# A diffusion block on one Trainium2 core: fewer and reordered first loads, the last sum of squares behind a weight split and a dot product, three dot products moved to a later stage, and an exponential table loaded ahead

## The chip, the core and the metric

The kernel runs on one core of a Trainium2 chip. The core has a matrix engine (PE in the profile; its weight loads, which overlap the matmuls, are PEld), VectorE (DVE), ScalarE (ACT), GpSimd (POOL) and SyncE (SP). Transfers between HBM and the core's memory are issued by an engine's queue, here nearly all by SP's, and are carried by 16 DMA engines. Each engine works through its own instructions in order, and waits for others by semaphores.

The metric is the device time of one execution in microseconds (us). Before the change three runs took 1520.72, 1521.96 and 1522.29 us; their median, 1521.96 us, is the time to compare with.

## The reference

One layer of a diffusion backbone: 256 latent tokens `x` and 256 context tokens `ctx`, width 2048, all float32. Cut to what matters here:

```python
mod = silu(c) @ w_mod + b_mod            # 6 x 2048: shifts, scales, gates; the same from c_ctx
h  = rms_norm(x, g_pre) * (1 + sc1) + sh1
hc = rms_norm(ctx, g_pre) * (1 + csc1) + csh1
# one projection w_in gives queries, keys and values of two mixers and two gates
oa = window attention with sinks (8 heads, 2 key heads, rotary)   # keys of h and hc
ob = neighbourhood attention (8 heads, relative bias)             # keys of h and hc
y  = (sigmoid(ga) * (oa @ w_br_a) + sigmoid(gb) * (ob @ w_br_b)) @ w_o
x  = x + gt1 * rms_norm(y, g_post)
x  = x + gt2 * rms_norm(conv_ffn(modulated rms_norm(x)), g_ffn_post)
```

The context enters only as keys and values. Every row of `w_mod` (2048 by 12288) is used once, against one or two vectors, so that part of the work is loading.

## The kernel before, in words

**Precision.** A float32 operand is split into two parts, a high one (`hi`, a rounded copy that ACT writes) and a low one (`lo = src - hi`, by DVE). A product is then three matmuls: high by high, low by high, high by low. `split` (L123) writes both parts; `halves` (L134) does it for a weight block of 128 by 2048 in two pieces, and leaves its last ACT and DVE instruction in `last`. So each weight block costs ACT and DVE two instructions each before PE can use it.

**Weights** arrive as raw blocks of 1024 KB or less in a ring of four buffers (`raw_block`, L113, tag `raw`). `load_to` issues the loads in the order in which the blocks are used, `block` (L162) splits one block ahead and loads two or three ahead. A buffer is free again when the block's low part has been made. The split parts have a ring of two (tags `wh`, `wl`), so the split of a block waits until PE has finished the block two before it.

**Dot products.** The parts of `w_mod` that aren't matmuls are multiply-and-sum instructions of DVE over 128 by 2048 elements: `dot` (L385) for the first shift columns, `beside` (L581) for the biases that the shifts give to the keys, and `mods` (L194), which takes one row block of `w_mod` (`wm_b`, 1024 KB through the same four raw buffers), and loads the next one ahead. 48 of these `mods` have to be done before the normalisation behind the attention, and 16 in the up projection.

**Stages.** The order of the work is that of the program text, planned by the language's scheduler with its own estimates, except where `manual_schedule` keeps the written order (PE up to L547, SP up to L439) and where `issue_after` puts an instruction behind another one on the same engine.

1. *Start.* SP issues, in order, `ccol` (16 KB, L101), the first scale block `wm_sc[0]` in four pieces (L278), the columns `cols` (80 KB, L291), the first input tile `xn` (256 KB), the first key weights `wk[0]` in three pieces (L293), `wm_sc[1]`, `wk[1]`, `xn[1]`. PE multiplies the identity with itself (`keep_busy`, L232) until `narrow` (L303) turns the scale block into 128 scale values, `evacuated` copies them (ACT), two small matmuls turn them into columns, and `scale_of` (L321) makes the column `Gc` (DVE) and the scaled input `hx`, `hc` in two parts (ACT, DVE).
2. *First keys,* the loop over k at L415: for each of 16 slices of the width, 36 matmuls add to six key heads (`keys`, L399). Inside, every second slice, the next two scale blocks are turned into scales and inputs, and `squares` (L341) adds the squares of two slices to `ssq` (one ACT instruction, two DVE additions). At k = 11 it is called for slices 12 and 13 and, in the same place, for 14 and 15 (L469), and behind them ACT loads the table for the square root (L471). At k = 12 the weights of slice 13 are split (`unit`, L364) and the first `dot` is placed. At k = 13 one matmul sums `ssq` over the partitions (L474), and `rstd_of` makes the inverse root.
3. *Second keys* (L493): four more key heads, and the shift columns.
4. *Values* (L602): three column groups in ten weight blocks numbered `nb`; beside them DVE does the key biases and then `mods`, 29 steps in all: 3 or 4 for a block, 1 for the last (L609).
5. *Queries and attention* (L669 to L767): per head a query block (`fill`), the scores, softmax with Exp on ACT, transposes and the product with the values. Before the loop two heads' queries are made (L747 to L753).
6. *Gates and branches* (L785): for each j of 16 output strips two gate blocks and one branch block, with `mods` one per gate, and one more beside the branch block at j of 4, 8, 11 and 13 (L799).
7. Output projection, first norm, up projection with convolution and gate, down projection, second norm.

Of the kernel before, what the change touches and what calls it, by code (L numbers as in the profile page):

```python
# [15 lines left out]
P = 128  # L16
# [42 lines left out]
def layer_kernel(ctx, tc, xc, xt, ccol, crow, wm_sc, wm_sd, wm_sh, wm_b, cols, wk, wkt, ws, rope, mask_a, bias_b, out):  # L59
# [41 lines left out]
    sync.dma_start(out=c2, in_=ccol)  # L101
# [138 lines left out]
    with ExitStack() as mx:  # L240
# [3 lines left out]
        with ExitStack() as at:  # L244
# [31 lines left out]
            def load_sc(k):  # L276
                if k < KT:
                    rsc[k] = raw_block(wm_sc[k], parts=1 if k else 4)  # L278
# [10 lines left out]
            load_sc(0)  # L289

            sync.dma_start(out=col[:, :C_CW], in_=cols[:, :C_CW])  # L291
            load_xn(0, 1)
            raws[0] = raw_block(*srcs[0], parts=3)  # L293
            load_sc(1)
            load_to(1)
            load_xn(1, 1)
# [17 lines left out]
            def evacuated(k, n, pm):  # L314
                ev = up.tile([P, 2 * P], F32, tag="half", bufs=2, name=f"ev{k}")
                e_ = nc.scalar.activation(ev[:, : n * P], pm[:, : n * P], AF.Copy)
                if k < 5:
                    queue[k] = (e_.ins, e_.ins)
                return ev

            def scale_of(k, n, ev):  # L321
# [11 lines left out]
                for t in range(k, k + n):  # L333
                    for v in range(2):
                        h_, x_, g_ = hh[v][:, t], xn[:, t, v * S : v * S + S], Gc[:, t, v : v + 1]
                        a_ = nc.scalar.activation(h_[:, 0], x_, AF.Copy, scale=g_)
# [4 lines left out]
            def squares(k, after):  # L341

                sq = sp.tile([P, 2, T2], F32, tag="sq", bufs=2, name=f"sq{k}")
                with tc.issue_after(after):
                    nc.scalar.activation(sq[:], xn[:, k : k + 2], AF.Square)
                if k:
                    nc.vector.tensor_tensor(out=sq[:, 0], in0=sq[:, 0], in1=sq[:, 1], op=ALU.add)
# [15 lines left out]

            def unit(u):  # L364
# [7 lines left out]
                for q in range(0, n, step):  # L372
                    split(h[:, q : q + step], h[:, n + q : n + q + step], raw[:, o + q : o + q + step], queue.get((u, q), queue.get(u)))
# [11 lines left out]
            def dot(after=None):  # L385
                t, v = divmod(ndot[0], 2)
                ndot[0] += 1
                with ExitStack() as es:
                    if after:
                        es.enter_context(tc.issue_after(after))  # L390
                    nc.vector.scalar_tensor_tensor(
                        out=rsd[t][:] if v else junk, in0=rsd[t][:], scalar=1.0, in1=shrow[v], op0=ALU.mult, op1=ALU.mult,
                        accum_out=sh0[:, t, v : v + 1])
                if v:
                    nc.vector.tensor_scalar(
                        out=shc[:, :, t], in0=sh0[:, t], scalar1=col[:, C_BMOD + t : C_BMOD + t + 1], scalar2=None, op0=ALU.add)
                    load_sd(t + 1)

# [12 lines left out]
            scale_of(0, 1, ev)  # L411
# [3 lines left out]
            for k in range(KT):  # L415
# [26 lines left out]
                if k in (12, 14):  # L442
                    dot(after)
                for i in range(NK1):
# [15 lines left out]
                    if n and i == first + 1:  # L460
# [7 lines left out]
                        if k == 11:  # L468
                            after = squares(14, done[0])  # L469
                            with tc.issue_after(done[0]):  # L470
                                warm_table(AF.Sqrt, "k", eps[:, 0:1])  # L471
# [131 lines left out]
            for c, (n0, nw, per) in enumerate(((0, 512, 4), (512, 512, 4), (1024, 256, 8))):  # L603
                pv = [acc(f"pv{c}_{i}") for i in range(4)]
                for g in range(KT // per):
                    wh, wl = block(2)
                    for kk in range(per):

                        if nb and kk < (1 if nb == 9 else 3 if nb % 2 else 4):  # L609
# [142 lines left out]
            fill(0)  # L752
            fill(1)  # L753
# [31 lines left out]
        for j in range(KT):  # L785
# [13 lines left out]
            mods(1 if j in (4, 8, 11, 13) else 0, crb[:])  # L799
# [376 lines left out]
```

## Time and profile before

| what | us |
|---|---|
| median of three runs | 1521.96 |
| the profiled execution | 1524.59 |
| its span (first to last instruction) | 1522.8 |
| PE busy | 1506.0 |
| PE's weight loads busy | 1318.1 |
| DVE busy | 1130.9 |
| ACT busy | 784.4 |

The profile is of one execution, taken by the hardware profiler. Times in it count from the start of the span. A timeline row gives the start, the duration, the engine, the line of the kernel and, in brackets, how long the engine stood idle before and what it waited for; rows of a queue carry a q behind the engine's name. A chain row gives start, duration and the work that the end of the run goes back to. A row of the waits gives the sum, the number and the longest of one kind of wait. A row of stretches gives the bounds, the length, the busy time of each engine with its number of instructions, the granted PE clock (1.00 is full speed), the share of the 16 DMA engines' time in use, and GB/s.

### The profile page before, as it was taken

The numbers are of one execution on the slowest core, as the hardware profiler recorded it, in microseconds if no ns is written. First come the engines' busy times: TensorE is split into PE (matmuls) and PEld (weight loads), VectorE is DVE, ScalarE is ACT, GpSimd is POOL, SyncE is SP. The second block draws the span as 40 slices with busy tenths as digits, with TensorE's granted clock in tenths as the row PEclk, the third lists the DMA queues.
The fourth block names the chain that finished last, engine by engine and source line by source line (L and its number), as shares of the span: only waits on it lengthen the run. The fifth ranks groups of instructions, "written<-read, shape, count | busy, mean of one in ns | idle before, by whom it ended". The sixth has DMA issues, their size and how long they took to land.

```text
span 1522.8 us, 22640 instructions
## 1 busy us (share of the span) xinstructions
PE 1506.0 (99%) x9044; PEld 1318.1 (87%) x9044; DVE 1130.9 (74%) x1673; ACT 784.4 (52%) x1280; POOL 1.6 (0%) x10
## 2 busy tenths in 40 slices
PE   8999999999999999999999999999999999999998
PEld 7988889899988888888888888888888888888886
DVE  3487797888888989887778887888888776444444
ACT  4342542676774445454476555555555555344342
POOL 0000000000000000000000000000000000000000
PEclk9999999999999999999999999999999999999999
DMA  9978778733358888888955666666666556655552
GB/s 350 389 271 328 291 283 326 265 112 130 136 204 322 329 325 337 332 327 317 380 218 195 248 233 237 248 231 221 243 246 235 208 194 234 235 194 193 193 194 83
DMA packets 59833, 382.19 MB, mean 251 GB/s; under 512 B 6608, under 2 KB 7376, under 8 KB 17488
## 3 DMA queue, kind: packets, MB, share of 16 engines
q1 hardware_dynamic: 59152, 379.70, 67.5%
q8 instruction: 71, 1.16, 0.3%
q10 hardware_dynamic: 576, 1.05, 0.2%
q14 instruction: 34, 0.28, 0.0%
HBM read 376.48 MB, written 4.24 MB: 250 GB/s over the span
## 4 chain that ended last, share of the span: by engine, by line
PE 94%; DMA 3%; DVE 2%; ACT 1%; issue 1%; SPq 0%; DVEq 0%; ACTq 0%
PE pu L174 21%; PE py_d L827 16%; PE pu L175 11%; PE pk L403 7%; PE pg L174 7%; PE py_o L827 5%; PE pv L616 5%; PE pq L174 4%; PE pb L174 4%; PE pg L175 4%; PE pb L175 2%; PE pq L175 2%; DMA raw<-in_wm_b_dram 2%; PE po L742 2%; PE s L712 1%; PE pm L309 1%
## 5 line engine op out<-in xcount | busy, mean ns | idle before, releaser
L131 DVE TENSOR_TENSOR wl<-raw,wh 128x1024 fp32r<-128x1024 f32 x444 | 529.4, 1221 | 232.6 <-ACT wh L127 232.4
L127 ACT ACTIVATE wh<-raw 128x1024 fp32r<-128x1024 f32 x444 | 453.1, 1054 | 293.1 <-PE py_d L827 129.0
L174 PE MATMUL pu<-h,wh 128*128 128x512 f32 x1408 | 488.5, 390 | 0.0
L175 PE MATMUL pu<-h,wl 128*128 128x256 f32 x1408 | 396.9, 282 | 0.0
L174 PEld LDWEIGHTS pu<-h,wh 128*128 128x128 f32 x1408 | 264.3, 188 | 55.5 <-DVE h L960 0.2
L175 PEld LDWEIGHTS pu<-h,wl 128*128 128x128 f32 x1408 | 266.1, 189 | 0.1
L827 PE MATMUL py_d<-wh,ff 128*128 128x512 f32 x704 | 216.8, 389 | 0.0
L174 PE MATMUL pg<-hx,wh 128*128 128x512 f32 x464 | 161.5, 390 | 0.0
L827 PEld LDWEIGHTS py_d<-wh,ff 128*128 128x128 f32 x704 | 132.1, 188 | 27.4
L204 DVE SCALAR_TENSOR_TENSOR raw<-raw,crb 128x2048 f32<-128x2048 f32 x64 | 146.2, 2285 | 9.3 <-DMA raw<-in_wm_b_dram 8.0
L827 PE MATMUL py_d<-wl,ff 128*128 128x512 f32 x352 | 136.9, 389 | 0.0
L175 PE MATMUL pg<-hx,wl 128*128 128x256 f32 x464 | 130.8, 282 | 0.0
L403 PE MATMUL pk<-hx,ku 128*128 128x256 f32 x480 | 117.8, 287 | 2.3 <-DVE ku L131 1.9
L403 PE MATMUL pk<-hc,ku 128*128 128x256 f32 x480 | 114.8, 281 | 0.0
L179 ACT ACTIVATE half_u<-pu 128x256 f32<-128x256 f32 x88 | 33.6, 384 | 152.7 <-PE pu L175 152.7
L174 PE MATMUL pq<-hx,wh 128*128 128x512 f32 x304 | 108.6, 396 | 0.0
L174 PEld LDWEIGHTS pg<-hx,wh 128*128 128x128 f32 x464 | 87.1, 188 | 18.2
L403 PEld LDWEIGHTS pk<-hx,ku 128*128 128x128 f32 x480 | 90.5, 189 | 7.7 <-issue 4.7
L403 PEld LDWEIGHTS pk<-hc,ku 128*128 128x128 f32 x480 | 90.7, 189 | 1.3 <-DVE hc L337 0.8
L174 PE MATMUL pb<-oab,wh 128*128 128x512 f32 x256 | 89.4, 390 | 0.0
L175 PEld LDWEIGHTS pg<-hx,wl 128*128 128x128 f32 x464 | 87.7, 189 | 0.0
L175 PE MATMUL pq<-hx,wl 128*128 128x256 f32 x304 | 85.7, 282 | 0.8 <-DVE wl L131 0.8
(184 smaller groups left out, 1937.8 us busy)
## 6 DMA issues: line engine op xcount, KB each, us to landing
raw<-in_ws_dram SPq DMA_DIRECT2D x222, 1024.0 KB, 4.9
raw<-in_wm_b_dram SPq DMA_DIRECT2D x64, 1024.0 KB, 5.1
raw<-in_wm_sc_dram SPq DMA_DIRECT2D x15, 1024.0 KB, 7.9
raw<-in_wm_sh_dram SPq DMA_DIRECT2D x16, 768.0 KB, 7.0
raw<-in_wkt_dram SPq DMA_DIRECT2D x10, 1024.0 KB, 5.5
crb<-sild SPq DMA_DIRECT2D x6, 1024.0 KB, 6.7
raw<-in_wk_dram SPq DMA_DIRECT2D x7, 768.0 KB, 8.4
sd<-in_wm_sd_dram SPq DMA_DIRECT2D x4, 1024.0 KB, 9.0
```

Of the source, the lines that this page charges most:

```text
L127: a_ = nc.scalar.activation(hi, src, AF.Copy)
L131: v_ = nc.vector.tensor_tensor(out=lo, in0=src, in1=hi, op=ALU.subtract)
L174: nc.tensor.matmul(pt[:, :], wh[:, w], a, start=first and i == 0, stop=False, skip_group_check=True)
L175: nc.tensor.matmul(pt[:, :S], wl[:, w], a[:, 0], start=False, stop=last and i == n - 1, skip_group_check=True)
L179: a_ = nc.scalar.activation(t[:], pt[:, S:], AF.Copy)
L204: nc.vector.scalar_tensor_tensor(out=r, in0=r, scalar=1.0, in1=row, op0=ALU.mult, op1=ALU.mult, accum_out=modx[:, j : j + 1])
L309: nc.tensor.matmul(pm[32 * j : 32 * j + 32, t * P : t * P + P], cc[:, q, :], rsc[k + t][:, q * P : q * P + P], start=q < 4, stop=q >= KT - ...
L403: nc.tensor.matmul(pk[:, v * S : v * S + S], wt[:, w], hh[v][:, k, a], start=k == 0 and a == 0 and wt is wh and v == 0, stop=k == KT - 1 a ...
L616: nc.tensor.matmul(pv[i][:, :nw], src[:, k, a, t0 : t0 + P], wt[:, w], start=k == 0 and q == 0, stop=k == KT - 1 and q == 2)
L712: nc.tensor.matmul(s_ps[:], qs[hd][:, a, qt * P : qt * P + P], k_[:], start=q == 0, stop=q == 2)
L742: nc.tensor.matmul(po[:, :S], v_[:, b], pTs[hd][:, b, a], start=b == 0 and q == 0, stop=b == 3 and q == 2)
L827: nc.tensor.matmul(py[t][:], act[:, k, a, t * P : t * P + P], wt[:, w], start=k == 0 and q == 0, stop=k == nk - 1 and q == 2)
```

## The change

- `ccol` is issued by ACT's queue and not by SP's. `wm_sc[0]` comes in two pieces in place of four, `wk[0]` in one in place of three and ahead of `cols` and `xn`; `xn[1]` comes ahead of `wk[1]`.
- In the start, the first `hx` is put behind the first `evacuated` on ACT, and the last third of the first weight split behind the first inputs.
- The squares of slices 14 and 15 move from k = 11 to k = 12, behind the split of the weights of slice 13: ACT's square behind ACT's part of that split, then the square-root table; on DVE the order is split, `dot`, additions. At k = 13 the copy of the last scales (ACT) is put behind the weight split of slice 14.
- In the values, block 8 has two steps beside it in place of four, and block 9 none in place of one: 26 steps, so three `mods` fewer. In the branches, j of 6, 9 and 10 have one `mods` more.
- One ACT instruction with Exp, and so its table load, is put behind the weight split of the second query block, ahead of the attention loop.

```diff
-    sync.dma_start(out=c2, in_=ccol)
+    nc.scalar.dma_start(out=c2, in_=ccol)
...
-                    rsc[k] = raw_block(wm_sc[k], parts=1 if k else 4)
+                    rsc[k] = raw_block(wm_sc[k], parts=1 if k else 2)
...
             load_sc(0)
+            load_to(0)
 
             sync.dma_start(out=col[:, :C_CW], in_=cols[:, :C_CW])
             load_xn(0, 1)
-            raws[0] = raw_block(*srcs[0], parts=3)
             load_sc(1)
+            load_xn(1, 1)
             load_to(1)
-            load_xn(1, 1)
...
             def evacuated(k, n, pm):
                 ev = up.tile([P, 2 * P], F32, tag="half", bufs=2, name=f"ev{k}")
-                e_ = nc.scalar.activation(ev[:, : n * P], pm[:, : n * P], AF.Copy)
+                with ExitStack() as es:
+                    if k == KT - 2:
+                        es.enter_context(tc.issue_after(done_u[k][0]))
+                    e_ = nc.scalar.activation(ev[:, : n * P], pm[:, : n * P], AF.Copy)
...
-                        a_ = nc.scalar.activation(h_[:, 0], x_, AF.Copy, scale=g_)
+                        with ExitStack() as es:
+
+                            if v == k == 0:
+                                es.enter_context(tc.issue_after(queue[0][0]))
+                            a_ = nc.scalar.activation(h_[:, 0], x_, AF.Copy, scale=g_)
...
-            def squares(k, after):
+            sq_ = []
+
+            def squares(k, after, behind=None):
...
-                    nc.scalar.activation(sq[:], xn[:, k : k + 2], AF.Square)
+                    sq_[:] = [nc.scalar.activation(sq[:], xn[:, k : k + 2], AF.Square).ins]
                 if k:
-                    nc.vector.tensor_tensor(out=sq[:, 0], in0=sq[:, 0], in1=sq[:, 1], op=ALU.add)
+                    with ExitStack() as es:
+                        if behind:
+                            es.enter_context(tc.issue_after(behind))
+                        nc.vector.tensor_tensor(out=sq[:, 0], in0=sq[:, 0], in1=sq[:, 1], op=ALU.add)
...
-                    split(h[:, q : q + step], h[:, n + q : n + q + step], raw[:, o + q : o + q + step], queue.get((u, q), queue.get(u)))
+                    done_u[u] = split(
+                        h[:, q : q + step], h[:, n + q : n + q + step], raw[:, o + q : o + q + step], queue.get((u, q), queue.get(u)))
...
-            scale_of(0, 1, ev)
+            done = scale_of(0, 1, ev)
+            queue[0, 4 * P] = done[:2]
...
-                if k in (12, 14):
+                if k == 12:
+
+                    d_ = dot(done_u[k + 1][1])
+                    after = squares(14, done_u[k + 1][0], d_)
+                    with tc.issue_after(sq_[0]):
+                        warm_table(AF.Sqrt, "k", eps[:, 0:1])
+                if k == 14:
                     dot(after)
...
-                        if k == 11:
-                            after = squares(14, done[0])
-                            with tc.issue_after(done[0]):
-                                warm_table(AF.Sqrt, "k", eps[:, 0:1])
...
-                        if nb and kk < (1 if nb == 9 else 3 if nb % 2 else 4):
+                        if nb and kk < (0 if nb == 9 else 2 if nb == 8 else 3 if nb % 2 else 4):
                             beside(1)
...
             fill(0)
+            with tc.issue_after(last[0]):
+                warm_table(AF.Exp, "e", eps[:, 0:1])
             fill(1)
...
-            mods(1 if j in (4, 8, 11, 13) else 0, crb[:])
+            mods(1 if j in (4, 6, 8, 9, 10, 11, 13) else 0, crb[:])
```

(`dot` now also returns its DVE instruction, so that others can be put behind it.)

More of the change, by code (lines that the diff above doesn't have):

```diff
@@ L362, in load_unit @@
                         in_=wk[k : k + 2, :, NK1 * P :].rearrange("k p n -> p k n"))
+            done_u = {}
             def unit(u):
@@ L390, in dot @@
                         es.enter_context(tc.issue_after(after))
-                    nc.vector.scalar_tensor_tensor(
+                    d_ = nc.vector.scalar_tensor_tensor(
                         out=rsd[t][:] if v else junk, in0=rsd[t][:], scalar=1.0, in1=shrow[v], op0=ALU.mult, op1=ALU.mult,
-                        accum_out=sh0[:, t, v : v + 1])
+                        accum_out=sh0[:, t, v : v + 1]).ins
                 if v:
@@ L397, in dot @@
                     load_sd(t + 1)
+                return d_
             def keys(pk, wh, wl, o, k):
```

## The prediction, made before the changed kernel was run

> **What bounds the kernel now.** I read the page first: which engine has no room.
>
> ```profile
> PE 1506.0 (99%) x9044; PEld 1318.1 (87%) x9044; DVE 1130.9 (74%) x1673; ACT 784.4 (52%) x1280; POOL 1.6 (0%) x10
> ...
> L204 DVE SCALAR_TENSOR_TENSOR raw<-raw,crb 128x2048 f32<-128x2048 f32 x64 | 146.2, 2285 | 9.3 <-DMA raw<-in_wm_b_dram 8.0
> ...
> raw<-in_wm_b_dram SPq DMA_DIRECT2D x64, 1024.0 KB, 5.1
> ```
>
> PE is busy in 1506.0 of 1522.8 us, and the change takes no matmul away. So it can win only the 16.8 us in which PE stands still, and what a lowered PE clock costs. The second view is therefore PE's waits:
>
> ```profile
> PE pk L403 <- DVE ku L131: 1.9, 1, 1.9
> PE pm L309 <- DMA raw<-in_wm_sc_dram: 1.6, 2, 0.9
> PE ptx L940 <- DVE yg L930: 1.4, 2, 1.0
> PE s L712 <- ACT q L127: 1.3, 1, 1.3
> PE pq L175 <- DVE wl L131: 0.8, 1, 0.8
> PE pk L403 <- ACT hx L336: 0.4, 1, 0.4
> ```
>
> The diff touches five of these six: the first key weights (0.4), the two scale blocks (1.6), the weights of slice 13 (1.9), the second query block (0.8) and the second query (1.3). The third row, in the norm, stays, as does the end of the run. After each of these waits PE runs without a gap to the next one, so what is won there lasts to the end, unless a new wait takes it back. I go through the places in order of price.
>
> **The wait at slice 13.** The timelines of DVE and of ACT, then the chain of waits around it:
>
> ```profile
> 82.26 0.68 DVE L347 TENSOR_TENSOR sq<-sq 128x512 f32<-128x512 f32 x1
> 82.98 0.69 DVE L348 TENSOR_TENSOR ssq<-ssq,sq 128x512 f32<-128x512 f32 x1
> 83.58 2.29 DVE L391 SCALAR_TENSOR_TENSOR kT<-sd,crb 128x2048 f32<-128x2048 f32 x1
> 85.80 0.95 DVE L131 TENSOR_TENSOR ku<-raw,ku 128x768 fp32r<-128x768 f32 x1
> ```
>
> ```profile
> 79.85 1.99 ACT L345 ACTIVATE sq<-xn 128x1024 f32<-128x1024 f32 x2
> 81.86 1.28 ACT L95 ACT_TABLE_LOAD   x1
> 83.26 0.83 ACT L127 ACTIVATE ku<-raw 128x768 fp32r<-128x768 f32 x1
> ```
>
> ```profile
> 74.02 1.89 PE pm L309 x64
> 75.90 0.90 PE pk L403 x6
> ...
> 86.81 0.50 PE pk L403 x2
> 87.31 2.99 PE pm L309 x64
> 90.30 1.40 PE pk L403 x6
> ...
> 93.54 0.86 PE pss L474 x2
> ```
>
> ```profile
> 84.88:86.81 1.93, 0.00 (x1) 0.01 (x1) 1.87 (x3) 0.00 (x0) 0.00 (x0) 1.00 0.84 265
> ...
> 87.24:91.31 4.07, 4.07 (x70) 3.67 (x70) 0.00 (x0) 0.96 (x2) 0.00 (x0) 0.58 0.87 260
> ```
>
> PE stops at 84.88 for 1.93 us, for the low part of slice 13's weights. ACT makes the high part only at 83.26, behind two squares and the table load; DVE puts the squares' additions and a dot product of 2.29 us ahead of the low part. Right behind the wait the granted clock is 0.58 in a stretch of 4.07 us: 64 matmuls take 2.99 for 1.89, the next six 1.40 for 0.90. That is 1.10 + 0.50 = 1.60 us more (by the clock, 0.42 x 4.07 = 1.71). The place costs 1.93 + 1.6 = about 3.55 us.
>
> With the new order ACT has one square ahead of the split, so the high part starts near 80.9 and ends at 81.7. DVE is then free at 82.26, and the low part is done by 83.2, 1.7 us ahead of PE's need at 84.88. Behind it come the dot product (to 85.5) and the last two additions (82.26 to 83.58 took 1.32, so to 86.8). What waits for that is the matmul over `ssq`: it stands at 93.54, and without stall and slow clock at 93.54 - 3.55 = 90.0. 3.2 us of cover. The table load ends near 84.2 and has nothing of PE behind it, since the weights of slice 14 can't be split before PE leaves slice 12. The last raw and square buffers come free up to 2 us later on SP's queue, but their loads are used only in the next stage. I take the whole 3.55; from below 0, if the wait only moves (first rival); from above 3.7.
>
> The page "TensorE: Matmul & The Clock Gate" of the Trainium skill (Part 1, and its table of goals) puts the fall to half speed behind an idle window of about 3.4 us, and advises against gaps over about 3 us. Here the clock fell behind 1.93 us, so the measurement decides; by the rule as written only 1.93 of the 3.55 would belong to this wait. The page also calls its window free-running, by which the same short wait need not always cost the clock, and the clock can fall without it (a rival below).
>
> **The query stage.** ACT's timeline, and one row of the chain:
>
> ```profile
> 274.76 0.63 ACT L127 ACTIVATE k<-kT 128x512 fp32r<-128x512 f32 x1 [2.81 <-DVE raw L204]
> ...
> 285.47 1.06 ACT L127 ACTIVATE wh<-raw 128x1024 fp32r<-128x1024 f32 x1 [0.57 <-DMA raw<-in_ws_dram]
> ...
> 288.49 1.28 ACT L721 ACT_TABLE_LOAD   x1
> ...
> 291.58 0.40 ACT L127 ACTIVATE q<-rq 128x256 fp32r<-128x256 f32 x1
> ```
>
> ```profile
> 275.60 9.84 DMA raw<-in_ws_dram
> ```
>
> PE's rows give the two waits as 0.8 and 1.3 us. For the first one: ACT stood idle 2.81 us until the ninth `mods` of the values was done, and split the key and the next block only then. With six `mods` in place of nine that wait is gone, and the split comes about 2.8 us earlier, more than 0.8. For the second: `q` is late because the table load of 1.28 stands in ACT's row, and because a weight block landed 9.84 us after its issue, behind `wm_b` blocks. Three blocks fewer are 3 x 1.05 MB, at 410 GB/s (the row for 10 to 27 us below) 7.7 us of loading that no longer stands ahead of it. 1.28 and 0.57 are already more than 1.3; and the 0.8 that PE comes earlier is covered by the 2.81. So up to 2.1 us; I take 2.0, from below 1.3 (the second wait's price alone). The Exp table then loads in a stretch in which PE has a whole query block to work on (as much as a third of the strip of 16.64 us below), and ACT the 2.81 us that it gains; its price is nothing while that holds, at most 1.28.
>
> **The start.** Rows of SP, then PE, then the chain, then stretches:
>
> ```profile
> 1.17 1.84 SPq L120 DMA_DIRECT2D raw<-in_wm_sc_dram  x4
> ```
>
> ```profile
> 7.13 0.43 PE L309 MATMUL pm<-raw,cc 128*32 128x128 f32 x8 [0.70 <-DMA raw<-in_wm_sc_dram]
> ...
> 9.62 0.39 PE L403 MATMUL pk<-hx,ku 128*128 128x256 f32 x1 [0.41 <-ACT hx L336]
> ```
>
> ```profile
> 5.43 7.98 DMA raw<-in_wm_sc_dram
> 13.45 1.08 PE pm L309 x32
> ```
>
> ```profile
> 8.00:10.00 2.00, 1.51 (x9) 1.15 (x9) 1.46 (x4) 1.63 (x5) 0.00 (x0) 1.00 0.82 315
> 10.00:27.00 17.00, 16.08 (x194) 14.35 (x194) 5.62 (x14) 5.62 (x14) 0.00 (x0) 1.00 1.01 410
> ```
>
> One issue on SP takes 1.84 / 4 = 0.46 us. The first scale block now starts 0.46 earlier, and the second is issued behind five transfers in place of nine on SP, from about 1.17 - 0.46 + 5 x 0.46 = 3.0 in place of 5.43. The bytes ahead of it stay; so its landing (5.43 + 7.98 = 13.41) moves by the 0.46, and by the hole of 0.18 x 2 = 0.36 in the stretch from 8 to 10, which a filled queue closes: to about 12.6. PE's first work moves 0.4 to 0.7 (the last piece of the scale block; `wk[0]` is ahead of `xn[0]`, so `hx` waits for the latter). PE, with a wait of 0.9 us ahead of 13.45 for this block, then gets to it at about 12.0 and goes on near 12.3. I take 1.2, with ends at 0.4 (the landing moves by the issue alone) and 2.0 (the three waits 0.7 + 0.4 + 0.9 all gone). The streams behind it run at full share (1.01), so a part may be lost later: second rival.
>
> **The branches.** Three `mods` return here:
>
> ```profile
> 572.01:588.65 16.64, 16.64 (x98) 14.75 (x97) 14.24 (x19) 8.26 (x13) 0.00 (x0) 1.00 0.83 316
> 588.65:605.29 16.64, 16.64 (x98) 14.73 (x97) 16.32 (x21) 8.37 (x13) 0.00 (x0) 1.00 0.99 375
> 605.29:621.90 16.61, 16.61 (x98) 14.74 (x96) 13.69 (x19) 8.53 (x14) 0.00 (x0) 1.00 0.85 314
> ```
>
> ```profile
> 601.38 1.22 DVE L131 TENSOR_TENSOR wl<-raw,wh 128x1024 fp32r<-128x1024 f32 x1
> ```
>
> One strip takes PE 16.64 us. The second row is j = 8, which has three `mods` already: DVE is busy in 16.32 us and the DMA share is 0.99, yet PE has no gap. Now j = 8 to 11 have three, one after the other, each with 2.29 us of DVE and 1024 KB of SP's loads more than in the first row. A weight's low part ends at 602.60, 2.7 us ahead of the next strip. So there is just room: I take 0, with a loss of up to 1.6 (third rival), and no gain.
>
> **Sum.** 3.55 + 2.0 + 1.2 - 0 = 6.75 us. The profiled execution, 1524.59, becomes 1517.8; the median of the runs lies 2.63 below the profiled one, and I take the same 6.75 off it: 1521.96 - 6.75 = 1515.2. A change of 0.2%, 3.0 us, is about what a measurement of this kernel can tell from none; the line lies at 1518.9.
>
> **Rivals.** *The wait at slice 13 only moves*: to the `ssq` matmul or to slice 14, whose split shares DVE with additions now made later. It needs 3.2 us of delay to begin. Then 3.55 is gone: 3.2 in all, 1518.8, right at the line. 0.12.
>
> *The start is lost in the loads*: the scale blocks land no earlier, because the DMA engines are full from 10 us on, and PE waits later for what it won. 5.55 in all, 1516.4. For it: share 1.01. Against it: the next two blocks are issued only when PE frees a buffer, so they move with PE. 0.10.
>
> *The branches become bound by the loads*: six blocks, 6.29 MB, for a strip. 316 GB/s at 0.83 and 314 at 0.85 are 381 and 369 at full share; at the lower one a strip takes 17.05 us, 0.41 more, in four strips 1.6: 5.15 in all, 1516.8. 0.07. The page "DMA: Bandwidth & Descriptors" of the Trainium skill (Where 436 GB/s comes from) lets HBM bind at about 358 GB/s for a core; by it the four strips would lose an estimated 3.7 us. The 410 and 375 GB/s above speak against it.
>
> *The clock falls all the same*, at another place: then the 1.6 us stay, 5.15 in all, 1516.8. Against it: the slow stretch stands right behind the longest wait of PE's rows and nowhere else before the end. 0.03.
>
> *Slower*: a moved dot product comes to the head of DVE's queue before its block has landed, and the weights' low part queues behind it. The page's row for L204 shows that this happens: 8.0 us of DVE waiting for `wm_b`. It decides from 2.7 us of waiting; if the block is issued only at the dot product's turn, 5.1 us pass. PE then waits 2.4 and loses 1.6 by the clock, in four strips 16: 1531. Against it: the next block is always loaded one ahead, and j = 8 shows nothing of it. 0.04.
>
> *The change doesn't do what it says*: the planner puts other work where the new order leaves room, and the table or the dot product stays ahead of the weights. The start alone, 1520.8. 0.04.
>
> **Numbers.** My forecast has 0.60: 1515.2, itself from 1514 to 1517. The second, third and fourth rival are faster too, and the first lies half on each side of the line: faster 0.60 + 0.10 + 0.07 + 0.03 + 0.06 = 0.86; same 0.06 + 0.04 = 0.10; slower 0.04. The range starts from all ends at their best (3.7 + 2.1 + 2.0 = 7.8, 1514.2), less 1.2, by which one of three runs lay under the median: 1513.0. Above it takes in the second to fourth rival and most of the first: 1519.0.
>
> **What would show it.** Right: PE's waits without the rows for `ku`, `s` and `pq`, the clock at 1.00 from 82 to 92 us, the `pm` row of 64 at 1.89 there, the second scale block's matmuls near 12.3, a table load of Exp ahead of the first scores with no PE wait behind it, no PE gap between 560 and 640 us. Wrong: a new wait of PE at L474 or on `ku` of slice 14; a wait on `wl` in the branches; scale blocks of later slices waited for.

## The result, and the profile after

| | median us | ratio to before, 95% interval |
|---|---|---|
| before (10 runs beside after) | 1522.35 | |
| after (10 runs) | 1525.47 | 1.0024 [1.0015, 1.0032] |

The change makes the kernel slower by 0.24%, 3.1 us; the forecast was 6.75 us faster. The profiled execution of after took 1525.5 us, with a span of 1523.4 us. First PE's waits in after, all that the view has:

```profile
PE ptx L961 <- DVE yg L951: 5.6, 2, 4.9
PE busy L236 <- POOL ident masks.py:199: 1.9, 1, 1.9
PE s L731 <- ACT q L127: 1.4, 1, 1.4
```

The waits for `ku`, `pm` and `pq` are gone, as forecast. The wait in the norm (`ptx`), which was to stay at 1.4, is 5.6 now. The scores' wait (`s`) is a new one: before, PE waited for the second head's `q` (1.34 us, at 292.04); that wait is gone, and now PE waits for the first head's (1.39 us, at 279.13). But the rows explain only a part: PE's waits add up to 8.9 us against 9.3 before, and the time is longer all the same.

The profiled execution of before stood 2.6 us above the median of the first three runs. A second profile of it was taken later (run e12 below, 1522.47 us, span 1520.7); against that one the starts of the stages stand so:

| first (or last) matmul | before, second profile | after | after minus before | the stage alone |
|---|---|---|---|---|
| 64 scale matmuls before the last | 74.17 | 72.95 | -1.2 | start -1.2 |
| sum of the squares (`pss`) | 93.77 | 88.58 | -5.2 | slice 13 -4.0 |
| first query block | 271.55 | 266.48 | -5.1 | values +0.1 |
| first gate block (`pg`) | 436.77 | 433.11 | -3.7 | queries +1.4 |
| output projection (`py_o`), first | 686.49 | 688.54 | +2.1 | branches +5.7 |
| output projection, last | 774.73 | 775.85 | +1.1 | -0.9 |
| up projection (`pu`), first | 784.45 | 787.38 | +2.9 | norm +1.8 |
| end of the span | 1520.69 | 1523.38 | +2.7 | rest -0.2 |

So the first third won 5.2 us, about what was forecast for the start and slice 13 (1.2 and 3.55), and then three places gave back 8.9 us: the queries, the branches, and the norm. The chain of waits of after shows the win at slice 13: the 64 scale matmuls take 1.88 (2.99 before), the six behind them 0.90 (1.40 before), with nothing between.

```profile
83.94 1.88 PE pm L309 x64
85.82 0.90 PE pk L419 x6
...
88.58 0.86 PE pss L493 x2
```

**The branches and the fillers.** The chain of after, further on, has rows that the chain of before has nowhere in the branches:

```profile
628.00 0.67 PE busy L236 x6
...
640.68 0.89 PE busy L236 x8
...
653.37 0.67 PE busy L236 x6
...
666.28 0.45 PE busy L236 x4
```

`busy` are the multiplications of the identity by itself. The program text asks for 26 of them (52 matmuls) behind the output projection, `keep_busy(26, "2")`, to keep PE's clock up while the norm is computed. They depend on nothing, so the planner may put them anywhere; it put 48 of the 52 into the branches, in groups of 4 to 8 (rows of four groups above), the other 4 among the output projection, and none into the norm. PE's timeline there, and a stretch of it:

```profile
775.85 0.39 PE L848 MATMUL py_o<-wl,zz 128*128 128x512 f32 x1
781.19 0.47 PE L961 MATMUL ptx<-ident,yg 128*128 128x128 f32 x1 [4.95 <-DVE yg L951]
```

```profile
779.50:786.30 6.80, 4.50 (x20) 4.10 (x21) 5.20 (x14) 5.59 (x14) 0.00 (x0) 0.50 0.78 313
```

PE stands still for 4.95 us, and the clock is at 0.50 for 6.80 us. Why the planner moved them isn't shown. The rows of the waits have none in the branches, but that doesn't mean that PE had its operands in time there: the fillers stand in those waits (e4_nofill below).

**The queries.** ACT's timeline of after:

```profile
273.08 0.36 ACT L179 ACTIVATE half_q<-pq 128x256 f32<-128x256 f32 x1
...
274.42 1.28 ACT L95 ACT_TABLE_LOAD   x1
...
275.93 0.84 ACT L255 ACTIVATE tr_q<-rq 64x256 f32<-64x256 f32 x2
...
278.68 0.40 ACT L127 ACTIVATE q<-rq 128x256 fp32r<-128x256 f32 x1
```

The Exp table is loaded in the middle of the chain that makes the first head's `q`: between `half_q` (its block is done) and the rotation `tr_q`. PE has its second query block done at 277.75 and waits 1.39 us for `q`.

### The profile page after: what moved, and what is told of

The parts are those of the page before. It is cut to its first block, busy times and chain, and to the rows that moved or that the text cites. A ratio compares the mean times of both kernels' runs of the same rounds, so it can differ in the third digit from the quotient of the medians.

```text
span 1523.4 us, 22639 instructions
## 1 busy us (share of the span) xinstructions
PE 1506.4 (99%) x9044; PEld 1318.9 (87%) x9044; DVE 1132.3 (74%) x1673; ACT 784.1 (51%) x1281; POOL 1.6 (0%) x10
## 4 chain that ended last, share of the span: by engine, by line
PE 98%; DVE 1%; ACT 0%; DMA 0%; issue 0%; DVEq 0%; ACTq 0%
PE pu L174 21%; PE py_d L848 16%; PE pu L175 11%; PE pk L419 8%; PE pv L635 7%; PE pg L174 7%; PE py_o L848 5%; PE pq L174 4%; PE pb L174 4%; PE pg L175 4%; PE pq L175 2%; PE pb L175 2%; PE po L761 2%; PE s L731 1%; PE pm L309 1%; PE pt L752 1%
## 5 line engine op out<-in xcount | busy, mean ns | idle before, releaser
L204 DVE SCALAR_TENSOR_TENSOR raw<-raw,crb 128x2048 f32<-128x2048 f32 x64 | 146.1, 2284 | 7.9 <-DMA raw<-in_wm_b_dram 4.9
```

The costliest lines, as they stand in the source:

```text
L204: nc.vector.scalar_tensor_tensor(out=r, in0=r, scalar=1.0, in1=row, op0=ALU.mult, op1=ALU.mult, accum_out=modx[:, j : j + 1])
```

## The experiments

All are compared with the kernel before on the same chip; its medians there lay between 1521.83 and 1522.58.

### e1_pin: the fillers held in the norm

```diff
-        keep_busy(26, "2")
+        with tc.issue_after(pe_end[0]):          # the last matmul of the output projection
+            keep_busy(26, "2")
```

> The changed kernel, with the 26 filler products ahead of the up projection put behind the last matmul of the output projection on PE. Theory A (the planner took the fillers out of the norm's gap and put them among the branches, where PE had no time to spare): no fillers and no gaps in the branches, the norm's gap filled, clock at full speed behind it; the 5.7 us of the branches, the 0.9 us of misplaced fillers of the output projection and the 1.2 us of the norm are won: about 7 us under the changed kernel, 1517 to 1519. Theory B (the three more dot products make PE wait in the branches, and the fillers only filled those waits): PE shows gaps of some 5 us in the branches, and only the norm's clock is won: 1522 to 1524.

1522.29 us, ratio 1.0002 [0.9994, 1.0011]: 3.2 us less than after. The norm is filled again and the clock stays up, and the output projection is 1.4 us shorter than before, since no filler stands among its matmuls now. But the branches still lose 4.7 us (start of `pg` to start of `py_o`). PE's waits make up 2.4 us of that (0.45, 0.73, 0.45 and 0.74); the rest lies in longer busy times of PE in the same strips, as the rows of e7_exp below show (17.61 and 17.46 us for 16.64). So the fillers were one fault, and not the larger one.

### e4_nofill: no fillers there at all

```diff
-        keep_busy(26, "2")
```

> The changed kernel without the 26 filler products ahead of the up projection (nothing of the result hangs on them). Theory A: the branches are 5.3 to 5.7 us shorter and without gaps, the norm idles as in the changed kernel and the clock falls behind it: 1519.5 to 1520.5. Theory B: gaps in the branches in place of fillers, time as the changed kernel: 1525.

1524.24 us, 1.0014 [1.0005, 1.0023]. The branches lose the same 4.7 as in e1_pin; with fillers they lost 5.7. So the fillers mostly filled waits that were there anyway, and cost 1.0 us there themselves. The norm has its wait of 4.95 us and the half clock, as in after. The 3.2 us between after and e1_pin are thus 1.2 for the fillers' presence at the wrong places (after to e4_nofill) and 1.95 for their absence from the norm (e4_nofill to e1_pin).

### e2_nodots and e3_dotsonly: the move of the dot products taken out, and alone

```diff
-  kk < (0 if nb == 9 else 2 if nb == 8 else 3 if nb % 2 else 4)      # values, in e2
+  kk < (1 if nb == 9 else 3 if nb % 2 else 4)
-  mods(1 if j in (4, 6, 8, 9, 10, 11, 13) else 0, crb[:])            # branches, in e2
+  mods(1 if j in (4, 8, 11, 13) else 0, crb[:])
```

e3 is the kernel before with the opposite edit.

> The changed kernel without the moved dot products (values and branches as before). Theory A: the fillers are back in the norm, all but a few; start and slice 13 stay won (1.1 and 3.9 us), the query stage is near the kernel before: 1517 to 1518.5. If instead the start, the slice or the table load made the norm late, the norm's wait of 5 us and the slow clock stay: 1521 or more.

> The kernel before with the moved dot products alone. Theory A: fillers among the branches, norm idle 5 us with half the clock behind it; 5.7 - 0.9 + 1.2 us more, less up to 0.8 in the query stage: 1526 to 1528. If another part of the change moved the fillers: no slower than before, 1520 to 1523.

Without the move 1517.80 us, 0.9973 [0.9963, 0.9983]; the move alone 1529.68, 1.0055 [1.0042, 1.0069]. Taken out of the change, the move of three dot products gives back 7.7 us (1525.47 to 1517.80); put into the kernel before, it costs 7.2. And it buys nothing: in e2 the wait for `pq` is gone too, with all nine `mods` still in the values (PE waits 0.8 us for the second head's `q` there). In e2 the fillers stand where they stood before the change; in e3 they are in the branches. So the move of the dot products also moved the fillers.

### e11_slice13 and e12_before_look: the order at slice 13 alone, and a second profile of before

e11 holds the diff's parts for `squares`, `done_u`, `dot` and the square-root table, and nothing else of it.

> The kernel before with the reordering around slice 13 alone (squares behind the weight split, dot product moved up, square-root table behind the square). Theory A, the forecast's sum: the wait of 1.93 us and the 1.6 us of half clock behind it both go in the ordinary execution, 1522.4 - 3.55 = 1518.9. Theory B: the half clock behind this wait was in the profiled execution of the kernel before (2.6 us above the median of its runs) and not in most others, so the wait alone goes: 1520.5. In both, PE has no wait at slice 13. Rival of the forecast: the wait only moves, 1521.5 to 1522.4.

> The kernel before once more, for a second profile of it. By theory A its clock falls to half behind the wait at slice 13 again (3.4 us at half speed near 88 us) and the span is near 1522.8. By theory B the wait of 1.9 us is there and the clock stays, with a span near 1520.

e11: 1518.46 us, 0.9976 [0.9966, 0.9986], that is 3.85 us less than the 1522.31 beside it. e12, one run: 1522.47 us. PE's waits in this second profile of before, then the stretch around slice 13:

```profile
PE busy L236 <- POOL ident masks.py:199: 1.9, 1, 1.9
PE pk L403 <- DVE ku L131: 1.9, 1, 1.9
PE ptx L940 <- DVE yg L930: 1.4, 2, 1.0
PE pm L309 <- DMA raw<-in_wm_sc_dram: 1.2, 1, 1.2
PE s L712 <- ACT q L127: 0.2, 1, 0.2
```

```profile
85.00:91.30 6.30, 4.38 (x70) 3.80 (x70) 1.91 (x3) 0.22 (x1) 0.00 (x0) 0.73 0.86 278
```

The wait at slice 13 is the same, and the clock was at half speed for 3.4 us behind it again (0.73 in the mean of these 6.3 us). But the wait for `pq` (0.8 in the first profile) isn't there, and that for `s` is 0.2 (1.3). The values' dot products explain the difference. DVE's timeline in the second profile:

```profile
260.24 2.29 DVE L204 SCALAR_TENSOR_TENSOR raw<-raw,crb 128x2048 f32<-128x2048 f32 x1 [2.62 <-DMA raw<-in_wm_b_dram]
...
269.67 2.29 DVE L204 SCALAR_TENSOR_TENSOR raw<-raw,crb 128x2048 f32<-128x2048 f32 x1 [0.44 <-DMA raw<-in_wm_b_dram]
```

The last of the nine starts at 269.67 here and at 272.42 in the first profile, where a block had landed later. So both waits of the query stage belonged to one execution, and the query stage had 0.2 us to win; the profile of e11, whose query stage is that of before, has the same 0.2.

### e7_exp: the Exp table behind head 0's values

```diff
-            with tc.issue_after(last[0]):
+            with tc.issue_after(v_end[0]):           # ACT's part of the split of head 0's values
                 warm_table(AF.Exp, "e", eps[:, 0:1])
```

The two lines also stand ahead of `fill(0)` now. This and the next runs have the pinned fillers.

> The changed kernel with the fillers pinned, and the Exp table load moved from ahead of head 0's last rope step to behind the split of head 0's values. Theory A: in the changed kernel the table load of 1.28 us stands in the chain that makes the first q, and the wait of 1.39 us ahead of the first scores is that load; moved, the wait goes, 1522.3 - 1.3 = 1521.0. Theory B: the first q is late for another reason (the rope chain itself, or the block), and the wait stays or only shrinks by 0.3: 1522.

1520.88 us, 0.9994 [0.9985, 1.0002], against 1.0002 [0.9994, 1.0011] for e1_pin. The intervals overlap; the traces separate the two: PE has no wait for `s` any more, and the stage from the first query block to the first gate block is 1.4 us shorter than in e1_pin. The table load of 1.28 us was the wait.

### e5_gated: the dot products behind the gate's addition

What the branches of e1_pin look like at strip 10. First DVE, then ACT:

```profile
628.98 2.29 DVE L204 SCALAR_TENSOR_TENSOR raw<-raw,crb 128x2048 f32<-128x2048 f32 x1
631.19 0.08 DVE L204 DVE_READ_ACCUMULATOR raw<-raw,crb 128x1 f32 x1
631.19 0.42 DVE L180 TENSOR_TENSOR g<-pg,half_g 128x256 f32<-128x256 f32 x1
633.04 2.36 DVE L131 TENSOR_TENSOR wl<-raw,wh 128x1024 fp32r<-128x1024 f32 x2 [1.43 <-ACT wh L127]
```

```profile
627.71 0.36 ACT L179 ACTIVATE half_g<-pg 128x256 f32<-128x256 f32 x1
631.64 0.42 ACT L804 ACTIVATE g<-g 128x256 f32<-128x256 f32 x1 [3.57 <-DVE g L180]
631.97 1.99 ACT L127 ACTIVATE wh<-raw 128x1024 fp32r<-128x1024 f32 x2
```

A chain over two engines: the dot product (L204) stands on DVE ahead of the addition that makes the gate (L180), the sigmoid on ACT waits 3.57 us for that addition, the next weights' high part is queued behind the sigmoid, and the low part behind the high one. The edit queues each of the branches' dot products behind the latest gate's addition:

```diff
-            mods(1 if ... else 0, crb[:])
+            with tc.issue_after(g_end[1]):           # DVE's addition for the gate
+                mods(1 if ... else 0, crb[:])
```

> The same seven dot products in the branches as in the changed kernel with the fillers pinned to the norm (that kernel took 1522.29, with PE waits of 0.45, 0.73, 0.45, 0.74 us at its strips 9 and 10 and some 4.7 us lost in the branches). Each dot product is now queued on DVE behind the addition that makes its strip's gate, in place of ahead of it. Theory A (order): the time is lost because a dot product of 2.29 us stands ahead of the gate's addition, ACT's sigmoid waits for that (3.57 us idle) and the next high part stands behind the sigmoid; turned round, the four PE waits are gone and 4 to 4.7 us come back: 1517.6 to 1518.3. Theory B (amount): three dot products in each of four strips following one another are simply more than DVE has room for (16.62 us busy in a stretch of 18.80); the order only moves the wait, 1521.5 to 1522.5, with PE waits on wl in the same strips. Theory C (loads): the blocks land too late; no change either, 1522, and the idle time ahead of the high parts is put down to the DMA.

1519.12 us, 0.9980 [0.9971, 0.9989]. The branches lose 3.2 in place of 4.7: the order is worth 1.5 us. That is short of theory A. (By the medians e5_gated is 3.2 us under e1_pin. The two profiles are 2.35 apart: 0.6 ahead of the queries, where the clock came up at 5.1 us in place of 7.5, and the rest, but for the 1.5, behind the branches.) ACT's idle times in the branches of e5_gated are now headed by another cause:

```profile
ACT wh L127 <- DMA raw<-in_ws_dram: 10.0, 10, 2.7
```

A likely reason, not tried: dot products that run later hold their raw buffer for longer, and the weight blocks come later.

### e6_spread, e9_alternate, e10_run3: the same seven dot products in other strips

`j in (4, 6, 8, 11, 13, 14, 15)` in e6_spread (from e1_pin); `j in (1, 3, 5, 7, 9, 11, 13)` in e9_alternate and `j in (2, 4, 6, 8, 9, 10, 13)` in e10_run3 (both from e7_exp).

> The changed kernel with the fillers pinned, and the seven extra dot products of the branches in strips 4, 6, 8, 11, 13, 14, 15 in place of 4, 6, 8, 9, 10, 11, 13: the same number, but nowhere three in strips that follow one another. Theory A (order in the strips 8 to 11): most of the 4.7 us comes back, 1518 to 1519.5, with small waits left where a dot product still stands ahead of a gate's addition (strip 8). Theory B as room over four strips in a row: all of it comes back, 1517.6. If the whole stage had too little room for DVE or for the loads: nothing comes back, 1522.

> The kernel with pinned fillers and moved Exp table (1520.88; 4.65 us lost in its branches, seen as pg first -7.85 against pb last -3.20), with the seven extra dot products in strips 1, 3, 5, 7, 9, 11, 13: never three dot products in two strips that follow one another, and none in strips 14 and 15, where they made the first output weights late (2.29 + 0.52 us of PE waits in the spread kernel). Theory D (debt): a strip of 16.6 us with three dot products overdraws DVE a little, a strip with two pays it back; the loss comes only when strips of three follow one another. All 4.65 come back: 1516.2, with no PE wait between 440 and 690 us. Theory B (amount over the whole stage): the same number of dot products, so 1520.9. Theory E: every strip of three costs its own 1.2 wherever it stands, 1520 to 1521.

> The same kernel with the seven extra dot products in strips 2, 4, 6, 8, 9, 10, 13: three strips of three in a row in place of four. Theory D (debt): a part of the loss is left, that of a run shorter by one: by the run of four, where the second strip of the run still went without a visible wait and the third and fourth lost 1.2 and 2.2 and the strip behind 1.2, a run of three loses 1.2 to 2.5: 1517.4 to 1518.7. If the loss is the same for every strip of three in a run: 3 of 4, 3.5 us, 1519.7. If only the order in one special strip matters (strip 11): nothing is left, 1516.2.

| | median us | ratio | lost between the first gate block and the output projection |
|---|---|---|---|
| e7_exp (strips 8 to 11 extra) | 1520.88 | 0.9994 [0.9985, 1.0002] | 4.65 |
| e10_run3 (8 to 10) | 1519.98 | 0.9984 [0.9975, 0.9993] | 3.7 |
| e9_alternate | 1518.28 | 0.9972 [0.9962, 0.9983] | 2.05 |
| e6_spread | 1522.21 | 1.0000 [0.9992, 1.0009] | 0.0 |

The loss goes with how the dot products lie and not with their number, so theory B is out. But the simple form of theory D is out as well: in e9_alternate no two strips of three follow one another, and two of them still lose about 1 us each. In e6_spread the strips lose nothing, and the time is no better, since the loss has moved to the first block of the next stage, behind the dot products of strips 14 and 15:

```profile
PE py_o L850 <- ACT wh L127: 2.3, 1, 2.3
...
PE py_o L850 <- DVE wl L131: 0.5, 1, 0.5
```

### e13_dot_noload and e14_load_nodot: VectorE's time against the loads

In e13 the dot products of strips 6, 9 and 10 read the row `crb` in SBUF in place of a loaded block; in e14 the blocks are loaded and the dot products go over 128 columns. So e13 leaves three columns of the modulation out, and e14 most of their terms. Both from e7_exp. The edit of e13:

```diff
+            if j in (6, 9, 10):
+                fake(crb[:])
+            else:
+                mods(1 if j in (4, 8, 11, 13) else 0, crb[:])
```

> The kernel with pinned fillers and moved Exp table (1520.88, of which 4.65 us are lost in the branches). The extra dot products of strips 6, 9 and 10 run over 128x2048 elements as before, but over the row of the condition that lies in SBUF; their three blocks of 1024 KB are not loaded (three columns of the modulation are left out). Theory L (loads): a raw buffer and 1 MB of loading for each extra dot product stand ahead of the weight blocks, which land late; without them the loss goes: 1516.2 to 1517. Theory V (VectorE): 2.29 us more of DVE in a strip that has 2 to 3 us of room, and the order they stand in, make the loss; it stays: 1520 to 1521.

> The same kernel, the other way round: the blocks of the dot products of strips 6, 9 and 10 are loaded as before, but the dot products go over 128 of the 2048 columns (three columns of the modulation are left out in most of their terms); all instructions of DVE stand in the same order. Theory L (loads): the loss stays, at least 3.5 of the 4.65 us: 1519.7 to 1521. Theory V (VectorE): three times some 2.1 us of DVE are gone, the strips 8 to 11 have room again, and the loss falls to 0 to 1.5: 1516.2 to 1517.7.

e13: 1515.87 us, 0.9961 [0.9948, 0.9975]; the branches lose nothing, and PE waits nowhere in them. e14: 1519.52 us, 0.9984 [0.9976, 0.9993]; they lose 3.6 of the 4.65. So it is theory L, if the loads are taken together with the buffers that they fill: shortening the three dot products gives back about 1.1 us in all, and without the blocks that come with them there is no loss.

Stretches by strip (from one strip's first branch matmul to the next one's), e7_exp first, strips 8 to 12, then e13, strips 8 to 11:

```profile
580.80:597.47 16.67, 16.67 (x100) 14.75 (x98) 15.46 (x18) 7.83 (x12) 0.00 (x0) 1.00 0.91 339
597.47:614.19 16.72, 16.72 (x100) 14.83 (x97) 15.43 (x22) 8.59 (x15) 0.00 (x0) 1.00 0.95 346
614.19:631.32 17.13, 17.13 (x99) 14.62 (x97) 14.33 (x19) 7.49 (x13) 0.00 (x0) 1.00 0.90 331
631.32:650.12 18.80, 17.61 (x97) 14.70 (x96) 16.62 (x21) 8.23 (x14) 0.00 (x0) 1.00 0.89 335
650.12:668.77 18.65, 17.46 (x99) 14.82 (x98) 17.93 (x21) 8.91 (x14) 0.00 (x0) 1.00 0.91 335
```

```profile
581.38:598.05 16.67, 16.67 (x99) 14.75 (x98) 16.35 (x21) 8.36 (x13) 0.00 (x0) 1.00 0.96 372
...
614.77:631.41 16.64, 16.64 (x98) 14.75 (x97) 16.48 (x21) 8.26 (x13) 0.00 (x0) 1.00 0.87 325
631.41:648.05 16.64, 16.64 (x98) 14.75 (x97) 15.20 (x20) 8.25 (x13) 0.00 (x0) 1.00 0.96 367
```

In e13 two strips have DVE busy for 16.35 and 16.48 of some 16.65 us, and PE doesn't wait: a full DVE alone is no loss. And in the losing strips of e7_exp (18.80 and 18.65 us) the DMA engines move 335 GB/s where they can move 367 to 372: they are not at their limit. How the loads are held back is read from SP's queue. Its issues in e7_exp, then in e13:

```profile
633.68 0.33 SPq L120 DMA_DIRECT2D raw<-in_ws_dram  x1
635.89 0.33 SPq L120 DMA_DIRECT2D raw<-in_wm_b_dram  x1
640.03 0.33 SPq L120 DMA_DIRECT2D raw<-in_ws_dram  x1
642.24 0.33 SPq L120 DMA_DIRECT2D raw<-in_wm_b_dram  x1
646.15 0.33 SPq L120 DMA_DIRECT2D raw<-in_ws_dram  x1
...
652.49 2.54 SPq L120 DMA_DIRECT2D raw<-in_ws_dram  x2
```

```profile
610.73 3.27 SPq L120 DMA_DIRECT2D raw<-in_ws_dram  x2
618.67 0.33 SPq L120 DMA_DIRECT2D raw<-in_wm_b_dram  x1
621.21 0.33 SPq L120 DMA_DIRECT2D raw<-in_ws_dram  x1
...
638.58 0.33 SPq L120 DMA_DIRECT2D raw<-in_ws_dram  x1
...
644.06 3.31 SPq L120 DMA_DIRECT2D raw<-in_ws_dram  x2
```

A strip needs three weight blocks (`ws`), so PE takes one in 16.64 / 3 = 5.55 us. In e13 they are issued so: seven of them from 610.73 to 644.06 (the row of 610.73 holds two, and two single ones are left out), six steps of 5.55. In e7_exp, in the strips with three dot products each, weight block and dot block alternate, and a weight block is issued every (652.49 - 633.68) / 3 = 6.27 us: three of them are 18.8 us, the length of the strip. The issues fall on the ends of the low parts (640.03 behind a low part that DVE's timeline has from 637.64 to 640.00, for example). SP's waits don't tell the two kernels apart. Their longest rows, for the stretch from 575 to 668 us, e7_exp and then e13, name different instructions of DVE:

```profile
SPq L120 <- DVE wl L131: 35.5, 11, 4.4
```

```profile
SPq L120 <- DVE bt L180: 19.9, 6, 4.9
```

But all rows of L120 together are 85.1 us in e7_exp, 81.5 in e13 and 84.2 in the kernel before (second profile), of 93: SP waits for a free buffer nearly all the time in each of them. What differs is the slack. In the strips of e7_exp that lose, the ring of four raw buffers turns without any: a block is issued only when DVE has emptied a buffer, it lands about 5 us later, ACT and DVE need some 7 us for it behind the other work, and only then the next one goes. The lead, the time from a block's landing to its split, shows how it came to that. A weight block had landed 7.5 us ahead of its split at strip 7 of e7_exp; for the next ones it was 5.5, 4.1, 2.5, 1.9 and 0.1 us, by strip 9, and in the strips that lose one block of three is split as it lands (0.0 us at 639.12, 0.2 at 657.53). In e13 the lead stays at 4 us or more up to strip 14. In the kernel before (second profile) it goes from 7.7 to 4.1 us around the strip with three dot products, and is back at 7.8 two blocks later. PE sees nothing of this until the lead is used up. That the loop is the cause is argued from these rows and not shown by a run. A fifth raw buffer, which would show it directly, wasn't tried. e14, whose dot products free their buffers 2.1 us earlier and still lose 3.6, leaves open how the loss divides between the bytes and the buffers. The loss lies there in strips 11 and 12, which have three whole dot products each, ahead of the gate's addition as in e7_exp.

### e8_nodots_pin_exp: the version that beats both

The change without the move of the dot products, with the pinned fillers and the Exp table behind head 0's values.

> All that the runs so far showed to win: the change without the move of the dot products (1517.8), with the fillers pinned behind the output projection (1.2 to 1.4 less, as py_o showed) and the Exp table behind head 0's values (0.8 less, the wait ahead of s that was left): 1515.5 to 1516.3 by theory A. Theory B: in this kernel the fillers stand in the norm already as they did before the change and the table costs nothing, so 1517.5 to 1518.

1515.97 us, 0.9960 [0.9948, 0.9972]: 6.6 us less than before. That it comes within 1 us of the time forecast for the change is chance, since the parts of the sum are others. Behind the first microseconds PE has one wait left, in the norm:

```profile
PE busy L236 <- POOL ident masks.py:199: 1.9, 1, 1.9
PE ptx L966 <- DVE yg L955: 0.6, 1, 0.6
```

## Why the prediction was wrong, point by point

**Slice 13: right.** Forecast 3.55; 4.0 in the trace of after, 3.85 alone by the medians of e11. The wait didn't move, to `pss` or to slice 14. That the clock's part was counted in was right too: it fell in both profiles of before, though not behind the same wait in e3 (last section), so an execution can have only the 1.9 us to win. By the rule of the Trainium skill's page "TensorE: Matmul & The Clock Gate" (Part 1, the window of about 3.4 us) only 1.93 would have belonged to this wait; the 3.85 measured decide against that reading.

**The start: right in the sum, but the step "The bytes ahead of it stay; so its landing [...] moves by the 0.46" failed, and the number is partly luck.** Forecast 1.2, measured 1.2; the second scale block's matmuls stand at 12.40 in the chain, where 12.3 was forecast. But the forecast landing of 12.6 by itself allows 0.8 us, and not the 12.3. The block landed 7.4 us after its issue at 3.17, near 10.6. It had landed at 13.41 and 12.11 in the two profiles of before, so its landing moved by 2.8 or 1.5 us, where its issue moved by 2.3. PE no longer waited for it, and came to it at its own pace. That pace hung on the clock, which reached full speed at 8.11 us in this execution, and at 5.98 and 5.52 in the two of before (in the second it fell again, from 8.93 to 12.35). In the eleven other profiles with the new start it came up between 5.09 and 8.03, and the same matmuls begin at 11.3 to 12.2; in the four with the old one at 13.2 to 13.6. So the start is worth 0.9 to 2.3 us, by the execution. The first work was not won: the chain of after begins with the row

```profile
0.73 4.37 DMA col<-in_ccol_dram
```

`ccol`, now on ACT's queue, landed at 5.11; from SP's queue it had been there at 2.34. The first scale piece, there at 4.94, waited for it, and PE began at 5.41 (5.23 before).

**The query stage: the step "So up to 2.1 us; I take 2.0" failed,** for two reasons. The 0.8 and 1.3 us that it was to win were waits of one execution, which lay 2.6 us above the median; in the second profile 0.2 us of them are left. That the price was there at all in the first one was bad luck in the choice of the execution. The prediction took 6.75 off the median of the runs as if the terms were the same there, and noted the 2.63 between the two without asking which term was in it. And of the Exp table it said "its price is nothing while that holds, at most 1.28". It held in that PE had a query block to work on; but the table stands in the chain that makes `q`, which was not slack. Price 1.4. The second head's wait went as forecast, and a wait of the first head came in its place. The stage lost 1.4 where 2.0 were to be won.

**The branches: the step "So there is just room: I take 0, with a loss of up to 1.6" failed,** and it is the largest: 4.7 us without the fillers, 5.7 with them. It argued from one strip with three dot products (DVE busy in 16.32 of 16.64, DMA share 0.99, no gap). That strip lived on the lead of the loads (7.7 us down to 4.1 in the second profile), and the next one had two dot products and paid it back. Four in a row are no four times the one. The third rival had the right resource, the loads, with a wrong price: it counted bytes at full share (0.41 us for a strip), where a strip lost up to 2.2 once the lead was gone. The estimate there from the page "DMA: Bandwidth & Descriptors" of the Trainium skill (Where 436 GB/s comes from: about 358 GB/s for a core), 3.7 us, comes nearer to 4.7, but not for its reason: strips without any loss ran at 372 and 367 GB/s, and those that lost at 335. The slower rival had a dot product wait for its block at the head of DVE's queue, and the weights behind it. The order is there (it is what e5_gated turned round, worth 1.5 us in the branches and not 16), but the dot products of these strips stand in the trace without such a wait.

**The norm: "The third row, in the norm, stays" failed.** It went from 1.4 to 5.6, and the clock fell there for 6.8 us. That the planner might put other work elsewhere was a rival (0.04), but only for the table and the dot product. Instructions that depend on nothing were not thought of. PE's last matmul ended at 776.24 and the clock fell at 779.5, 3.3 us later; here the trace is close to the window of about 3.4 us of the Trainium skill's page "TensorE: Matmul & The Clock Gate" (Part 1).

**The sum.** Forecast -3.55 - 2.0 - 1.2 + 0. Measured, by the table above, -4.0 + 1.4 - 1.2 + 5.7, and +0.8 for output projection, norm and what lies around them: +2.7 in the span, 3.1 in the medians.

## What to carry to other kernels

A strip that has no gap may be living on loads that are ahead of it: before work with loads of its own is added to several strips in a row, follow how far ahead of their use the blocks land, and count the time in which the ring of buffers turns, not the bytes alone. Work without dependencies that is meant for one gap has to be tied to that gap, or a change elsewhere moves it. And a wait of a few tenths of a percent should be seen in two profiles before a change is priced on it, above all if the profiled execution isn't at the median.

## What the runs showed of the hardware that was not expected

The same wait at slice 13 does not always cost the clock. In e3_dotsonly PE waits 1.9 us there as before, and the stretch around it reads

```profile
80.00:92.00 12.00, 10.08 (x128) 9.27 (x127) 8.19 (x14) 6.38 (x11) 0.00 (x0) 1.00 0.82 274
```

at 1.00, where both profiles of before had half speed for 3.4 us. The clock's records fit a grid: within each of the sixteen profiles all its changes lie whole steps of 3.41 us apart, and inside the kernel it is low for one step (3.41) or two (6.82, in the norms of after, e3 and e4). The waits of the two profiles of before (84.88 to 86.81, 85.05 to 86.97) lie whole within one step, and the clock falls at its end (87.90, 87.44). In e3_dotsonly a step ends inside the wait (84.66 to 86.58, the step at 85.97), and the clock stays. What tells these three apart is where the wait lies in the grid; how much idle time in a step is enough isn't shown.

A small transfer of 16 KB took 1.6 us from its issue on SP's queue, alone, and 4.4 us on ACT's queue, issued at the same time as the first half of a 1024 KB block on SP's (4.1 to 4.4 in all twelve profiles that have it there); which of the two, the queue or the company, makes the difference wasn't tried. And two executions of one kernel differed by 2.3 us in the query stage alone (167.5 and 165.2 from its first block to the first gate block), where a dot product's block landed later in the one.
